# Hybrid mixer and mixture-of-experts layer: low parts of the merged sum first in the last output block, two weight slots in their space, expert tiles in that of the router and of the F ring

## The chip, the cores and the metric

The kernel runs on one core of a Trainium2 chip. The metric is the device time of one execution in microseconds (us); smaller is better. A kernel's time is the median of several runs.

## What is computed

One layer of a trunk over 512 latent tokens of width 1024, with 256 context tokens. Three token mixers (pooling, differential attention, RWKV-7) give three branches, which are merged with gates; an output projection of the merged sum is added to the stream; then a router picks for each token one group of experts out of four and the best two experts in it, and the two experts' outputs are added to the stream.

```python
def merge_branches(branches, gates, w_br, w_out):
    ...
    return merged @ w_out

def hier_moe(h, w_rg, w_re, w_g, w_u, w_d):
    ...                      # top-1 group of 4, top-2 of its 8 experts
    # block_ffn, for each expert e and its tokens:
    return (jax.nn.silu(xblk @ w_g[e]) * (xblk @ w_u[e])) @ w_d[e]

x = x + mod[:, 2] * mix_l                      # mix_l = merge_branches(...)
f_l = modulate(x, norm2_g[l], mod[:, 3], mod[:, 4])
x = x + mod[:, 5] * hier_moe(f_l, ...)
```

There are 32 experts; each has a gate and an up matrix of 1024 x 512 and a down matrix of 512 x 1024, all in 4-byte floats, so 6 MiB an expert and 192 MiB in all. Every expert is computed for 64 token slots.

## The kernel before

**Stages.** Up to about 892 us the input projection, the mixers and the merge run. From there the output projection runs (`out_mm`, line 1440), in four blocks of 256 output columns; each block is done for four groups `t` of 128 tokens. The merged sum is kept as a rounded high part `mgh` and a remainder `mgl`, and the weights of a block as `wo[i][0]` and `wo[i][1]` likewise; one group of one block takes 24 matmuls, for each of the eight pieces `k` of the inner dimension high by high, low by high and high by low. `out_add` (lines 1446 to 1452) adds the result to the stream `xt2` on VectorE. In the loops at lines 1553 to 1574 blocks 2 and 3 are mixed with the router: `turned` (line 1363) transposes the stream of a token group into a tile `fT`, `logits` (line 1370) multiplies it with the router's weights, `route` (lines 1374 to 1395) finds the experts, `count` (line 1403) the place of each token in its expert, and `normed` (lines 1428 to 1435) writes the normalised tokens to a tile `xn` and, through a tile `xf` and the ACT queue, to the array `x_d` in the chip's memory. `gates` (lines 1408 to 1421) is the router's last step. `gather(0)` (lines 1494 to 1525) picks the rows of the first four experts by matmuls (line 1500) and writes them to `xT`; for later groups of four the rows come from `x_d` by an indirect DMA (line 1535).

**Experts.** The loop at line 1701 runs over the experts: `up` (line 1602) multiplies `xT` with the gate matrix, then with the up matrix, `hidden` applies the activation, `turn_` transposes, `down` (line 1637) multiplies with the down matrix of the expert before, `combine` and `add` (lines 1645 to 1647) put the result back to the tokens.

**Expert weights.** Every matrix is loaded as two halves of 1 MiB (128 rows of 8 KB). `order` is the order of loads: the order in which the experts use them, but for two halves, 4 and 5 (`SPARE`, expert 0's down matrix). `fetch(n)` issues loads on the SP queue up to the n-th; load n goes to the slot `RING[n % 13]`. So 13 loads fit in the ring and two more in `SPARE` tiles: 15 halves before the experts begin. A load waits, on SP and in SP's order, until its slot's earlier user is through:

- slots 0 to 7 lie in `pea`, slot 12 in two tiles of the ring named F;
- slots 8 and 9 (`ew8`, `ew9`) lie in the space of `mgh`, pieces k = 0 to 3 and 4 to 7;
- slots 10 and 11 lie in the pool `peq`, which is opened at line 1588 after the pools of `mgl` (`mgx`) and of five F tiles (`pf_`) are closed; the F tiles hold at that time the four `fT` and then the four `xf`, from which `x_d` is written;
- the two `SPARE` halves go to the tiles `oh`, `yhl` and `xT` of the pool `ep` (line 1591), which the experts use later, and which lies where the router's tiles were, and beyond.

```python
RING = (4, 5, 6, 7, 12, 0, 1, 2, 3, 8, 9, 10, 11)
...
fetch(11)          # line 1583: slots 8 and 9
gates()
...
fetch(NS)          # line 1589: slots 10 and 11; NS is 13
```

**Order.** A planner with a model of the time puts the instructions of each engine into an order, by their place in the program and by the priorities given (`tc.high_priority`); it also places all semaphores. Each engine and each DMA queue then runs its list in order.

Of the kernel before, what the change touches and what calls it, by code (L numbers as in the profile page):

```python
# [77 lines left out]
def trunk_kernel(ctx: ExitStack, tc: tile.TileContext, I, out, dbg=None, upto=99):  # L78
# [65 lines left out]
    def ps_big(shape=(128, 512)):  # L144
        return ppool.tile(list(shape), FT, name="pp", bufs=5)
# [4 lines left out]
    def ps_sm(shape=(128, 512)):  # L150
        return psum.tile(list(shape), FT, name="psm", bufs=3)
# [588 lines left out]

    pb = ctx.enter_context(ExitStack())
    TW = dict(bufs=1, reuse_waits="tile")
    pf_ = ctx.enter_context(ExitStack())

    wfb = ctx.enter_context(tc.tile_pool(name="rmapg", side="right", **TW))
    wfa = pf_.enter_context(tc.tile_pool(name="rmapf", side="right", **TW))

    class Ring:
        n = 0
# [738 lines left out]
    def gather(b):  # L1488

        oh = (ep if b else xnp).tile([128, 4, EB, 64], FR, name="oh", bufs=1)  # L1490
        ohf = oh.rearrange("p t e s -> p t (e s)")

        def chosen(t):
            return V.tensor_tensor(oh[:, t], slot[:, t, b * EB:b * EB + EB, None].to_broadcast([128, EB, 64]),
                                   io1[:, None, :].to_broadcast([128, EB, 64]), OP.is_equal)

        def rows_of(p, k, ts):
            for t in ts:
                for a in range(2):
                    PE.matmul(p, xns[t // 2][:, a, t % 2, k * 128:k * 128 + 128], ohf[:, t], start=(t == 0 and a == 0),  # L1500
                              stop=(t == 3 and a == 1))

        def put(k, p):
            if k % 2:
                S.activation(xT[:, k], p, AF.Identity, scale=g2c[:, k:k + 1], bias=s2c[:, k:k + 1])
            else:
                V.tensor_scalar(xT[:, k], p, g2c[:, k:k + 1], s2c[:, k:k + 1], op0=OP.mult, op1=OP.add)

        if b == 0:

            ahead = {}
            for t in range(3):
                chosen(t)
                yield
            for k in range(AH):
                ahead[k] = ps_big()[:, 0:EB * 64]
                rows_of(ahead[k], k, range(3))
            chosen(3)
            yield
            xT = ep.tile([128, KD, EB * 64], FT, name="xT")  # L1520
            for k in range(KD):
                p = ahead[k] if k in ahead else ps_big()[:, 0:EB * 64]
                rows_of(p, k, (3,) if k in ahead else range(4))
                put(k, p)
            yield xT, *slots(b, oh)
            return
        for t in range(4):
            chosen(t)
        yield
        gc, ix = slots(b, oh)  # L1530
        ii = ep.tile([128, EB // 2], U32, name="ii")
        V.tensor_copy(ii, ix)
        fe = fes[b % 2]
        for q in range(EB // 2):
            G.indirect_dma_start(out=fe[:, q], out_offset=None, in_=x_d[:, :],
                                 in_offset=bass.IndirectOffsetOnAxis(ap=ii[:, q:q + 1], axis=0),
                                 bounds_check=L - 1, oob_is_err=False)
        yield
        xT = ep.tile([128, KD, EB * 64], FT, name="xT")
        for k in range(0, KD, 2):  # L1540
            p = ps_big()
            for i in range(2):
                for q in range(EB // 2):
                    c = 2 * i + q
                    PE.transpose(p[:, c * 128:c * 128 + 128], fe[:, q, (k + i) * 128:(k + i) * 128 + 128], ident)
            for i in range(2):
                put(k + i, p[:, i * 256:i * 256 + 256])
            if k == 2:
                yield
        yield xT, gc, ix  # L1550

    nxt = gather(0)
    for t in range(4):
        p = ps_big()[:, 0:256]
        for k in range(KD):
            out_mm(p, wo[2], t, k)
        turned(t, 0, 4)
        out_add(p, t, 2)
    for t in range(5):
        if t < 4:  # L1560
            p = ps_big()[:, 0:256]
            for k in range(KD):
                out_mm(p, wo[3], t, k)
            out_add(p, t, 3)
        if t:
            with tc.high_priority(0):
                turned(t - 1, 4, 4)
                logits(t - 1, 0, 8)
                if t > 1:
                    count(t - 2)  # L1570
                route(t - 1)
            normed(t - 1)
        if t > 1:
            next(nxt)
# [5 lines left out]
    if upto < 7:  # L1580
        return
    dump("slot", slot)
    fetch(11)
    gates()
    m2x.close()
    mgx.close()
    pf_.close()
    peq = ctx.enter_context(tc.tile_pool(name="expq", side="right", **TW))
    fetch(NS)
    epx = ctx.enter_context(ExitStack())  # L1590
    ep = epx.enter_context(tc.tile_pool(name="experts", bufs=2, reuse_waits="tile"))
# [7 lines left out]
    def up(xT, w, pg, i):  # L1599
        for k in range(KD):  # L1600
            for h in range(2):
                PE.matmul(pg[64 * h:64 * h + 64, i], xT[:, k], of(w[i], k)[:, h * 256:h * 256 + 256],  # L1602
                          start=(k == 0), stop=(k == KD - 1), tile_position=(0, 64 * h))

    def hidden(pg, pool):
# [40 lines left out]
        PE.matmul(p, oT[:, t * 128:t * 128 + 128], yl, start=False, stop=True)  # L1646
        V.tensor_add(xt2[t][:, sl], xt2[t][:, sl], p)  # L1647

    def parts_of(y, h, rows, pool, name="yhl", eng=G):

        sl = slice(h * 512, h * 512 + 512)
        yhl = pool.tile([rows, 2, 512], FR, name=name, bufs=1)
        yh, yl = yhl[:, 0], yhl[:, 1]
        S.activation(yh, y[:, sl], AF.Copy)  # L1654
        eng.tensor_sub(yl, y[:, sl], yh.bitcast(FT))  # L1655
        return sl, yh, yl

    def combine(y, ix, last=False):

        oT = oT_  # L1660
        V.tensor_scalar(oT, iol, ix, None, op0=OP.is_equal)
        if last:
            yield
            with tc.high_priority(100):
                pts = [parts_of(y, h, 128, ep, *(("oh", G) if h else ("yhl", V))) for h in range(2)]
            for h in range(2):
                sl, yh, yl = pts[h]
                for t in range(4):
                    add(oT, t, sl, yh, yl)
                    (nc.sync if t % 2 else nc.scalar).dma_start(out[t * 128:(t + 1) * 128, sl], xt2[t][:, sl])  # L1670
            return
        pt_ = parts_of(y, 0, 128, ep)
        yield
        for t in range(4):
            add(oT, t, *pt_)
        pt_ = parts_of(y, 1, 128, ep)
        yield
        for t in range(4):
            add(oT, t, *pt_)
# [1 line left out]
    def store(t):  # L1681
        nc.sync.dma_start(out[t * 128:(t + 1) * 128], xt2[t])

    load(SPARE[0], *(ep.tile([128, 1, D], FT, name=nm, bufs=1) for nm in ("oh", "yhl")))
    load(SPARE[1], ep.tile([128, 2, D], FT, name="xT"))
    cur = next(nxt)
    io_ = xnp.tile([128, 2, L], FR, name="oh", bufs=1)
    iol, oT_ = io_[:, 0].bitcast(FT), io_[:, 1]
# [12 lines left out]
    for e in range(NE + 1):  # L1701
        fetch(NS + max(0, 6 * e - 2) - (2 if e > 1 else 0))
        j = e % EB
        if e < NE:
            if j == 0:
                got[e // EB] = cur
                nxt = gather(e // EB + 1) if e + EB < NE else iter(())
            xT = got[e // EB][0][:, :, j * 64:j * 64 + 64]
            pg = ps_big().rearrange("p (i n) -> p i n", i=2)
            up(xT, weights(e), pg, 0)  # L1710
        elif com:
            next(com, None)
# [33 lines left out]
    with tc.If(nmost > 64):  # L1746
        for t in range(4):
            if t % 2 == 0:
                xns.append(xnp.tile([128, 2, 2, D], FR, name=f"xn{t // 2}"))
            xf = op_.tile([128, D], FT, name="xf")  # L1750
            nc.sync.dma_start(xf, x_d[t * 128:(t + 1) * 128])
            S.activation(xns[-1][:, 0, t % 2], xf, AF.Copy)
            V.tensor_sub(xns[-1][:, 1, t % 2], xf, xns[-1][:, 0, t % 2].bitcast(FT))
        with tc.For_i(0, NE, 1) as e:
# [12 lines left out]
            with tc.For_i(0, 7, 1):  # L1767
# [18 lines left out]
                y = op_.tile([64, D], FT)  # L1786
                pg = ps_big().rearrange("p (i n) -> p i n", i=2)
                up(xT, wo, pg, 0)
                up(xT, wo, pg, 1)
                down(turn_(hidden(pg, op_), op_), wo, gc, y, 0)  # L1790
                oT = op_.tile([64, 512], FR)
                pt = ps_sm()[0:64]
# [1 line left out]
                    PE.transpose(pt[:, t * 128:t * 128 + 128], oh[:, t].bitcast(FT), ident)  # L1794
                S.activation(oT, pt, AF.Copy)
                for h in range(2):
                    pt_ = parts_of(y, h, 64, op_)
                    for t in range(4):
                        add(oT, t, *pt_)
        for t in range(4):  # L1800
# [115 lines left out]
```

## Time and profile before

| | |
|---|---|
| median of 3 runs | 1446.18 us |
| the runs | 1446.18, 1440.47, 1446.46 us |
| profiled execution | 1446.82 us, of it 1444.7 us in the span of the trace |
| busy in the span | TensorE 1362.9 us (94%), VectorE 819.1 us, ScalarE 483.4 us, GpSimd 382.9 us |
| moved by DMA | 401.00 MB, mean 278 GB/s |
| granted TensorE clock, mean | 0.979 of full speed (2.4 GHz) |

The trace is that of one execution, so a sum is made against 1446.82 us, of which 2.1 us lie outside the span. All positions are microseconds from the start of the span. "PE" is TensorE's matmuls, "PEld" its weight loads, DVE VectorE, ACT ScalarE, POOL GpSimd; SPq and ACTq are the engines' DMA queues. A matmul's end is modelled, so "busy" of PE says that the engine had work, not that it ran at its peak. DMA share is the mean busy share of the 16 DMA engines.

### The profile page before, as it was taken

To read this page: it belongs to the slowest core of one execution; us is meant where nothing else is said; L and a number is where in the kernel's file an instruction comes from. 1 tells how busy PE (TensorE), PEld (TensorE's weight loads), DVE (VectorE), ACT (ScalarE), POOL (GpSimd) and SP (SyncE) were. 2 spreads that over 40 slices of the span, in tenths; PEclk is the share of its full clock that TensorE was granted. 3 is DMA by queue.
4 is the path that set the end of the run, shared out by engine and by line. 5 is a ranking of instruction groups with operands and counts; after the bars stand their busy time and mean duration, and the time that the engine had idled before them with its cause. 6 is when DMAs were issued, how large, how long until landed. Compare 5 with 4: busy or idle time off the path is not lost.

```text
span 1444.7 us, 24038 instructions
## 1 busy us (share of the span) xinstructions
PE 1362.9 (94%) x9148; PEld 1019.1 (71%) x9148; DVE 819.1 (57%) x1670; ACT 483.4 (33%) x1089; POOL 382.9 (27%) x345
## 2 busy tenths in 40 slices
PE   5999999999999998899999998999999999999897
PEld 3786788987888886788887777985555554555443
DVE  4553327779988948367776886462333433333324
ACT  4432235765565632243345524341111111111101
POOL 2111155445532442212221347111101101111001
PEclk9999999999999999899999999999999999999999
DMA  9368655666566466985847276579999999999996
GB/s 367 150 216 312 233 181 171 217 216 222 168 231 208 183 207 209 243 259 143 259 135 245 88 266 232 192 292 417 418 416 418 418 417 418 418 417 419 418 418 245
DMA packets 138614, 401.00 MB, mean 278 GB/s; under 512 B 38821, under 2 KB 69541, under 8 KB 107776
## 3 DMA queue, kind: packets, MB, share of 16 engines
q1 hardware_dynamic: 102640, 332.72, 62.5%
q10 hardware_dynamic: 32256, 58.47, 11.0%
q0 software_dynamic: 3600, 8.24, 1.7%
q8 instruction: 74, 1.21, 0.3%
q14 instruction: 44, 0.36, 0.1%
HBM read 344.47 MB, written 58.72 MB: 279 GB/s over the span
## 4 chain that ended last, share of the span: by engine, by line
PE 62%; DMA 21%; DVE 9%; issue 4%; ACT 2%; POOL 1%; SPq 1%; ACTq 0%; DVEq 0%; POOLq 0%
PE pp L219 13%; PE pp L1602 8%; DMA ew<-in_w_eu_dram 7%; PE pp L233 4%; PE pp L1637 4%; PE pp L1146 3%; PE pp L1440 3%; DMA ew<-in_w_ed_dram 3%; DMA ew<-in_w_eg_dram 3%; PE sc L1001 2%; PE pp L832 2%; PE pp L1645 1%; PE pp L820 1%; PE sc L1000 1%; PE pp L865 1%
## 5 line engine op out<-in xcount | busy, mean ns | idle before, releaser
L1602 PE MATMUL pp<-ew,xT 128*64 128x256 f32 x1888 | 225.1, 383 | 15.3 <-DMA ew<-in_w_eu_dram 10.1
L1602 PEld LDWEIGHTS pp<-ew,xT 128*64 128x64 f32 x1888 | 131.9, 137 | 98.5 <-issue 17.9
L219 PE MATMUL pp<-xlh,wh 128*128 128x512 f32 x344 | 137.2, 410 | 6.0 <-ACT wide L412 6.0
L219 PE MATMUL pp<-xll,wh 128*128 128x512 f32 x344 | 136.8, 398 | 0.4 <-POOL xll L319 0.4
L219 PE MATMUL pp<-xlh,wl 128*128 128x512 f32 x344 | 136.1, 396 | 0.0
L1655 POOL TENSOR_TENSOR yhl<-m,yhl 128x512 fp32r<-128x512 f32 x30 | 38.2, 1274 | 364.9 <-ACT yhl L1654 364.9
L214 POOL TENSOR_TENSOR wl<-wraw,wh 128x512 fp32r<-128x512 f32 x84 | 114.0, 1386 | 61.9 <-ACT wh L213 54.9
L1647 DVE TENSOR_TENSOR x<-x,pp 128x512 f32<-128x512 f32 x128 | 80.8, 681 | 44.4 <-PE pp L1646 44.4
L1637 PE MATMUL pp<-ew,hT 128*64 128x512 f32 x440 | 101.3, 599 | 0.0
L1608 DVE TENSOR_TENSOR hh<-hh,pp 128x256 f32<-128x256 f32 x32 | 13.5, 421 | 148.0 <-ACT hh L1607 148.0
L219 PEld LDWEIGHTS pp<-xlh,wh 128*128 128x128 f32 x344 | 65.4, 192 | 26.0 <-ACT wide L412 6.7
L1640 DVE SCALAR_TENSOR_TENSOR m<-pp,gc,m 64x512 f32<-64x512 f32 x62 | 46.5, 750 | 62.5 <-PE pp L1637 61.8
L213 ACT ACTIVATE wh<-wraw 128x512 fp32r<-128x512 f32 (+1 forms) x112 | 61.0, 612 | 49.2 <-PE pp L219 47.0
L219 PEld LDWEIGHTS pp<-xll,wh 128*128 128x128 f32 x344 | 66.0, 192 | 15.4 <-issue 2.0
L219 PEld LDWEIGHTS pp<-xlh,wl 128*128 128x128 f32 x344 | 65.9, 191 | 14.1
L1637 PEld LDWEIGHTS pp<-ew,hT 128*64 128x64 f32 x440 | 28.9, 136 | 55.5 <-issue 50.7
L233 PE MATMUL pp<-wh,xlh 128*128 128x256 f32 x192 | 60.2, 314 | 3.4 <-ACT qo L658 2.3
L1616 ACT ACTIVATE hT<-psm 128x256 f32<-128x256 f32 x32 | 12.3, 384 | 152.1 <-PE psm L1614 146.3
L801 POOL TENSOR_TENSOR ao<-ar,cst 128x512 f32<-128x512 f32 x24 | 31.1, 1295 | 115.9 <-PE pp L813 46.3
L1607 ACT ACTIVATE hh<-pp 128x256 f32<-128x256 f32 x32 | 12.3, 384 | 139.6 <-PE pp L1602 139.6
L233 PE MATMUL pp<-wl,xlh 128*128 128x256 f32 x192 | 58.3, 304 | 0.0
L233 PE MATMUL pp<-wh,xll 128*128 128x256 f32 x192 | 58.2, 303 | 0.0
(436 smaller groups left out, 3126.3 us busy)
## 6 DMA issues: line engine op xcount, KB each, us to landing
ew<-in_w_eg_dram SPq DMA_DIRECT2D x59, 1024.0 KB
ew<-in_w_eu_dram SPq DMA_DIRECT2D x58, 1024.0 KB
ew<-in_w_ed_dram SPq DMA_DIRECT2D x56, 1024.0 KB
wraw<-in_w_in_dram SPq DMA_DIRECT2D x27, 1024.0 KB
u_d<-ub ACTq DMA_DIRECT2D x16, 1152.0 KB
wada<-in_w_adr_dram SPq DMA_DIRECT2D x16, 1024.0 KB
ar<-u_d SPq DMA_DIRECT2D x24, 640.0 KB
wa<-in_w_ad_dram SPq DMA_DIRECT2D x8, 1024.0 KB
```

Of the source, the lines that this page charges most:

```text
L213: S.activation(self.h[:, kk, :n], raw[:, kk, :n], AF.Copy)
L214: (eng[q % 2] if type(eng) is tuple else eng).tensor_sub(self.l[:, kk, :n], raw[:, kk, :n], self.h[:, kk, :n].bitcast(FT))
L219: PE.matmul(ps, a[:, k, cs], b[part][:, k], start=(k + n == 0), stop=(k == KD - 1 and n == 2))
L233: PE.matmul(ps, a[part][:, k, ts], b[:, k], start=(n == 0), stop=(n == 3 * KD - 1))
L801: G.tensor_mul(ao, aa[:, :, 2:3].to_broadcast([128, 4, 2, 64]), offm[:, None].to_broadcast([128, 4, 2, 64]))
L1146: PE.matmul(ps, a[:, k], bs[k][:, x], start=(c == 0), stop=(c == 11))
L1440: PE.matmul(p, a[:, ts], x[:, k], start=(k == 0 and c == 0), stop=(k == KD - 1 and c == 2))
L1602: PE.matmul(pg[64 * h:64 * h + 64, i], xT[:, k], of(w[i], k)[:, h * 256:h * 256 + 256], start=(k == 0), stop=(k == KD - 1), tile_position= ...
L1637: PE.matmul(pd[64 * h:64 * h + 64], hT[:, k], of(w[2], k)[:, h * 512:h * 512 + 512], start=(k == 0), stop=(k == 3), tile_position=(0, 64 * h))
L1640: V.scalar_tensor_tensor(y[ps_, h * 512:h * 512 + 512], pd[64 * h:64 * h + 64], gc, m5[ps_, h * 512:h * 512 + 512], op0=OP.mult, op1=OP.mult)
L1647: V.tensor_add(xt2[t][:, sl], xt2[t][:, sl], p)
L1655: eng.tensor_sub(yl, y[:, sl], yh.bitcast(FT))
```

## The change

- In block 3 the products low by high are taken out of the group loop and done first, ahead of block 2, into four accumulators `pss`; block 3's loop then does only high by high and high by low, 16 matmuls a group instead of 8 + 16. Block 2's accumulators for t = 1 to 3 come from the other accumulator pool. No matmul is added or removed.
- `mgx` is closed right behind block 2, and `peq` opened in its space; slots 10 and 11 come ahead of 8 and 9 in `RING`, and their loads (`fetch(11)`) are issued ahead of block 3.
- The F tiles' pool stays open. `xT` is kept as two halves in F tiles (two sets, four tiles), the fifth F tile takes half a `SPARE` load and then `yhl`. `ep` becomes smaller by these.
- The second `SPARE` load goes out as two transfers of 512 KB instead of one of 1 MiB.
- In the branch for more than 64 tokens an expert, tiles come from F as well; the trace of before shows no work of that branch.

```diff
@@ -740,10 +740,9 @@
-    pf_ = ctx.enter_context(ExitStack())
...
-    wfa = pf_.enter_context(tc.tile_pool(name="rmapf", side="right", **TW))
+    wfa = ctx.enter_context(tc.tile_pool(name="rmapf", side="right", **TW))
@@ -1217,7 +1216,7 @@
-    RING = (4, 5, 6, 7, 12, 0, 1, 2, 3, 8, 9, 10, 11)
+    RING = (4, 5, 6, 7, 12, 0, 1, 2, 3, 10, 11, 8, 9)
@@ -1501,10 +1500,11 @@
         def put(k, p):
+            x = xT[k // 4][:, k % 4]
...
-            xT = ep.tile([128, KD, EB * 64], FT, name="xT")
+            xT = xTs[b % 2]
@@ -1550,18 +1550,27 @@
     nxt = gather(0)
+
+    pss = [ps_big()[:, 0:256] for _ in range(4)]
     for t in range(4):
-        p = ps_big()[:, 0:256]
+        for k in range(KD):
+            PE.matmul(pss[t], mgl[k][:, t * 128:t * 128 + 128], wo[3][0][:, k], start=(k == 0), stop=False)
+    for t in range(4):
+        p = (ps_sm() if t else ps_big())[:, 0:256]
         for k in range(KD):
             out_mm(p, wo[2], t, k)
         turned(t, 0, 4)
         out_add(p, t, 2)
+    mgx.close()
+    peq = ctx.enter_context(tc.tile_pool(name="expq", side="right", **TW))
+    fetch(11)
     for t in range(5):
         if t < 4:
-            p = ps_big()[:, 0:256]
             for k in range(KD):
-                out_mm(p, wo[3], t, k)
-            out_add(p, t, 3)
+                for c in range(2):
+                    PE.matmul(pss[t], mgh[k][:, t * 128:t * 128 + 128], wo[3][c][:, k], start=False,
+                              stop=(k == KD - 1 and c == 1))
+            out_add(pss[t], t, 3)
@@ -1580,15 +1589,15 @@
-    fetch(11)
     gates()
     m2x.close()
-    mgx.close()
-    pf_.close()
-    peq = ctx.enter_context(tc.tile_pool(name="expq", side="right", **TW))
     fetch(NS)
     epx = ctx.enter_context(ExitStack())
     ep = epx.enter_context(tc.tile_pool(name="experts", bufs=2, reuse_waits="tile"))
+
+    spare = wfa.tile([128, 1, D], FT, name="F", bufs=7 - FB)
+    xTs = [[wfa.tile([128, KD // 2, EB * 64], FT, name="F", bufs=7 - FB) for _ in range(2)] for _ in range(2)]
+    yhl_ = []
@@ -1681,8 +1695,8 @@
-    load(SPARE[0], *(ep.tile([128, 1, D], FT, name=nm, bufs=1) for nm in ("oh", "yhl")))
-    load(SPARE[1], ep.tile([128, 2, D], FT, name="xT"))
+    load(SPARE[0], ep.tile([128, 1, D], FT, name="oh", bufs=1), spare)
+    load(SPARE[1], *(x.rearrange("p (o k) n -> p o (k n)", o=1) for x in xTs[1]))
...
```

## Rows read from the trace of the kernel before

**Rows 1.** Windows of the expert stage: length, busy us of PE, PEld, DVE, ACT, POOL, clock, DMA share, GB/s

```profile
966.50:1169.00 202.50, 200.88 (x1407) 113.75 (x1408) 77.69 (x146) 28.16 (x58) 27.11 (x23) 1.00 1.02 417
1169.00:1402.00 233.00, 217.62 (x1460) 116.72 (x1458) 82.09 (x148) 29.12 (x61) 25.99 (x22) 1.00 1.01 418
```

**Rows 2.** Chain that ended last, expert stage: start, us, what

```profile
1027.89 3.45 PE pp L1602 x32
...
1084.05 3.45 PE pp L1602 x32
...
1384.33 17.45 DMA ew<-in_w_eu_dram
1401.82 1.95 PE pp L1602 x16
```

**Rows 3.** Windows of DMA ahead of the experts, same columns as in Rows 1

```profile
926.00:940.00 14.00, 14.00 (x122) 14.00 (x121) 5.70 (x18) 5.68 (x14) 0.55 (x1) 1.00 0.01 4
...
946.00:957.50 11.50, 10.98 (x91) 10.16 (x89) 9.78 (x57) 6.61 (x12) 0.60 (x2) 1.00 0.91 331
957.50:959.50 2.00, 1.72 (x16) 1.60 (x16) 1.76 (x11) 0.16 (x1) 0.00 (x0) 1.00 0.04 14
959.50:971.00 11.50, 11.50 (x102) 10.05 (x103) 6.45 (x16) 3.98 (x6) 3.56 (x2) 1.00 0.96 372
```

**Rows 4.** Timeline of the SP queue: start, us, engine, line, operation

```profile
919.40 0.33 SPq L1251 DMA_DIRECT2D ew<-in_w_eu_dram  x1
919.78 0.95 SPq L1251 DMA_DIRECT2D ew<-in_w_eg_dram  x1
946.22 0.33 SPq L1251 DMA_DIRECT2D ew<-in_w_eg_dram  x1
948.54 10.76 SPq L1251 DMA_DIRECT2D ew<-in_w_eu_dram  x2
959.41 0.36 SPq L1251 DMA_DIRECT2D ew<-in_w_ed_dram  x1
959.90 0.35 SPq L1251 DMA_DIRECT2D oh<-in_w_ed_dram  x1
...
968.50 0.34 SPq L1251 DMA_DIRECT2D ew<-in_w_ed_dram  x1
...
981.51 5.84 SPq L1251 DMA_DIRECT2D ew<-in_w_eg_dram  x2
```

**Rows 5.** Waits of the SP queue, 900 to 1000: total us, times, longest

```profile
SPq L1251 <- PE pp L1440: 43.9, 4, 25.4
...
SPq L1251 <- DMA x_d<-F: 10.0, 1, 10.0
```

**Rows 6.** Timeline of PE: block 2's first matmul, the transposes behind its first group, two later steps

```profile
919.33 0.28 PE L1440 MATMUL pp<-xn,ew 128*128 128x256 f32 x1
...
922.18 0.60 PE L1363 MATMUL psm<-cst,x 128*128 128x128 f32 x4
...
962.57 1.06 PE L1738 MATMUL psm<-rt,cst 128*128 128x32 f32 x8
...
966.51 3.24 PE L1602 MATMUL pp<-ew,xT 128*64 128x256 f32 x28
```

**Rows 7.** Two windows as in Rows 1, and the sum of 919.3 to 966.5

```profile
935.50:948.50 13.00, 13.00 (x115) 13.00 (x114) 8.26 (x30) 8.17 (x15) 1.64 (x3) 1.00 0.30 101
948.50:960.30 11.80, 11.00 (x89) 10.06 (x88) 10.63 (x59) 5.62 (x11) 0.55 (x1) 1.00 0.75 276
...
sum 47.20, PE 46.40 PEld 45.34 DVE 27.86 ACT 20.01 POOL 2.47; mean PE 7.73 PEld 7.56 DVE 4.64 ACT 3.33 POOL 0.41
```

**Rows 8.** Timeline of DVE: block 3's first addition, the router's last step

```profile
935.53 0.42 DVE L1446 TENSOR_TENSOR tm<-pp,m 128x256 f32<-128x256 f32 x1 [1.42 <-PE pp L1440]
...
959.59 0.28 DVE L1421 TENSOR_TENSOR tg<-oo 128x128 f32<-128x128 f32 x1
```

**Rows 9.** A window behind the load issued at 919.40, same columns as in Rows 1

```profile
920.00:922.00 2.00, 2.00 (x19) 2.00 (x19) 0.57 (x2) 0.51 (x2) 0.00 (x0) 1.00 0.73 193
```

More of the change, by code (lines that the diff above doesn't have):

```diff
@@ L1503, in put @@
         def put(k, p):
+            x = xT[k // 4][:, k % 4]
             if k % 2:
-                S.activation(xT[:, k], p, AF.Identity, scale=g2c[:, k:k + 1], bias=s2c[:, k:k + 1])
+                S.activation(x, p, AF.Identity, scale=g2c[:, k:k + 1], bias=s2c[:, k:k + 1])
             else:
-                V.tensor_scalar(xT[:, k], p, g2c[:, k:k + 1], s2c[:, k:k + 1], op0=OP.mult, op1=OP.add)
+                V.tensor_scalar(x, p, g2c[:, k:k + 1], s2c[:, k:k + 1], op0=OP.mult, op1=OP.add)
         if b == 0:
@@ L1538, in gather @@
         yield
-        xT = ep.tile([128, KD, EB * 64], FT, name="xT")
+        xT = xTs[b % 2]
         for k in range(0, KD, 2):
@@ L1601, in up @@
             for h in range(2):
-                PE.matmul(pg[64 * h:64 * h + 64, i], xT[:, k], of(w[i], k)[:, h * 256:h * 256 + 256],
+                PE.matmul(pg[64 * h:64 * h + 64, i], xT[k], of(w[i], k)[:, h * 256:h * 256 + 256],
                           start=(k == 0), stop=(k == KD - 1), tile_position=(0, 64 * h))
@@ L1647, in add, with parts_of @@
         V.tensor_add(xt2[t][:, sl], xt2[t][:, sl], p)
-    def parts_of(y, h, rows, pool, name="yhl", eng=G):
+    def parts_of(y, h, yhl, eng=G):
+        if yhl is yhl_:
+            if not yhl_:
+                yhl_.append(wfa.tile([128, 2, 512], FR, name="F", bufs=7 - FB))
+            yhl = yhl_[0]
         sl = slice(h * 512, h * 512 + 512)
-        yhl = pool.tile([rows, 2, 512], FR, name=name, bufs=1)
         yh, yl = yhl[:, 0], yhl[:, 1]
@@ L1664, in combine @@
             with tc.high_priority(100):
-                pts = [parts_of(y, h, 128, ep, *(("oh", G) if h else ("yhl", V))) for h in range(2)]
+                pts = [parts_of(y, h, ep.tile([128, 2, 512], FR, name="oh", bufs=1) if h else yhl_, G if h else V)
+                       for h in range(2)]
             for h in range(2):
@@ L1671, in combine @@
             return
-        pt_ = parts_of(y, 0, 128, ep)
+        pt_ = parts_of(y, 0, yhl_)
         yield
@@ L1675, in combine @@
             add(oT, t, *pt_)
-        pt_ = parts_of(y, 1, 128, ep)
+        pt_ = parts_of(y, 1, yhl_)
         yield
@@ L1707, in trunk_kernel @@
                 nxt = gather(e // EB + 1) if e + EB < NE else iter(())
-            xT = got[e // EB][0][:, :, j * 64:j * 64 + 64]
+            xT = [got[e // EB][0][k // 4][:, k % 4, j * 64:j * 64 + 64] for k in range(KD)]
             pg = ps_big().rearrange("p (i n) -> p i n", i=2)
@@ L1749, in trunk_kernel @@
                 xns.append(xnp.tile([128, 2, 2, D], FR, name=f"xn{t // 2}"))
-            xf = op_.tile([128, D], FT, name="xf")
+            xf = wfa.tile([128, D], FT, name="F", bufs=7 - FB)
             nc.sync.dma_start(xf, x_d[t * 128:(t + 1) * 128])
@@ L1785, in trunk_kernel @@
                 V.tensor_copy(gc, pi)
-                y = op_.tile([64, D], FT)
+                y = wfa.tile([128, D], FT, name="F", bufs=7 - FB)[0:64]
                 pg = ps_big().rearrange("p (i n) -> p i n", i=2)
-                up(xT, wo, pg, 0)
-                up(xT, wo, pg, 1)
+                up([xT[:, k] for k in range(KD)], wo, pg, 0)
+                up([xT[:, k] for k in range(KD)], wo, pg, 1)
                 down(turn_(hidden(pg, op_), op_), wo, gc, y, 0)
@@ L1796, in trunk_kernel @@
                 for h in range(2):
-                    pt_ = parts_of(y, h, 64, op_)
+                    pt_ = parts_of(y, h, wfa.tile([128, 2, 512], FR, name="F", bufs=7 - FB)[0:64])
                     for t in range(4):
```

## Prediction

> **What bounds the kernel now.** I read the page's slices first, then windows, then the chain. From 966.5 us, where the first expert starts, the 16 DMA engines are full: share 1.02 and 417 GB/s up to 1169, 1.01 and 418 GB/s up to 1402 [rows 1]. The reader is to see that PE also looks busy there, but that the chain that ended last changes: up to about 1169 its pieces are PE's, an expert taking (1084.05 - 1027.89) / 4 = 14.0 us, and the last wait for a weight ends at 1401.82, behind a piece that is a DMA's from 1384.33 on [rows 2]. One expert's weights, 6 x 1.0486 MB at 418 GB/s, take 15.05 us, over PE's 14.0. So the stage is set by DMA: PE begins with 15 halves in store, eats them up, and then follows the transfers. The end moves by as much as the unbroken stream of weights is moved, and by nothing else. So the question is where that stream begins, and what it has behind it when it begins.
>
> It begins at 959.5. Between 926 and 940 the DMA engines stand nearly still (4 GB/s), from 946 to 957.5 they carry 331 GB/s, from 957.5 to 959.5 14 GB/s, and then 372 GB/s up to 971 [rows 3]. The SP queue tells why. After the load of 919.78 nothing goes out until 946.22 (slot 8) and 948.54 (slot 9), then nothing until 959.41 (slots 10 and 11), then the two SPARE loads from 959.90 on, and the first slot that an expert gives back is filled at 968.50 [rows 4]. SP waited at line 1251 for the output projection's matmuls 25.4 us at the longest, and once 10.0 us for the write `x_d<-F` [rows 5]: that is the place of slots 10 and 11, which must wait for the last `xf`.
>
> **The change, part by part.**
>
> *Loads for slots 10 and 11 (two halves, 2.51 us each) leave earlier.* One group of block 2 takes 24 matmuls in 922.18 - 919.33 = 2.85 us, 0.119 us each [rows 6]. Block 3's 32 low products, put first, take 3.8 us, so block 2's four groups end at 932.0 + 3.8 = 935.8 (932.0 is 919.33, four times 2.85, and some 0.4 for each of the three sets of transposes between them). `mgl`'s first four pieces are last read some 13 matmuls before that, at 934.3. So the two loads leave at about 934.4 and 936, in place of 946.22 and 948.54 for the tenth and eleventh, into idle DMA, and are in by 942. Behind them on SP stand only the loads of slots 8 and 9, which wait for block 3's end (948.54) anyway; ACT's queue, with the writes of `x_d`, is not SP's.
>
> *Slots 8 and 9 take the next two loads,* at block 3's end as before. So from 946 to 957.5 the same bytes flow as before: two halves, the writes of `x_d`, a constant. The wait of 10.0 us on `x_d` is gone.
>
> *What is late next.* The SPARE loads: `oh` lies where the router's tiles were, whose last reader ends at 959.59 + 0.28 = 959.87 [rows 8], and before, `oh` was issued at 959.90 [rows 4], so this very wait already ended last for it. The F tiles' last user (`x_d`, up to 958.9, by the 10.0 us behind 948.9) is earlier. So they still leave at 959.9. Behind them the ring is full: 13 + 2 halves are all there is room for, before and after, and the next load leaves only when expert 0 gives back its first half, at 968.50 [rows 4].
>
> *So the gain is not two loads (5.0 us) but the queue that stood at 968.50.* Before: from 959.5 to 971 flowed 11.5 us x 372 GB/s = 4.28 MB [rows 3]; the four halves are 4.19 MB, so they end 0.2 us before 971, at 970.8, and the stream goes on unbroken. At 418 GB/s they need 10.0 us, so the first of them began in effect at 960.8, 1.4 us behind its issue at 959.41. The load of 919.40 gives 1.7: by 922 it had moved 2 x 193 = 0.39 MB, 0.9 us of full rate [rows 4, 9]. I take 1.4, since it is the same stage; the range is 1.4 to 1.7. After: the SPARE halves flow from 961.3 to 966.3, the engines then idle, and the stream begins with the load of 968.50 at 969.9 (970.2 by the other price). It begins 970.8 - 969.9 = 0.9 us earlier (0.6 at least), if expert 0 starts when it did.
>
> The Trainium skill, DMA: Bandwidth & Descriptors, section "Latency and other measured facts", gives about 0.6 us to the first byte for queues of this kind. By it the stream would begin at 969.1, and the gain would be 1.7 us; the rows, with 1.4 and 1.7 us to the full rate, don't bear that out.
>
> *Is the stream unbroken afterwards?* The ninth load behind 968.50 leaves at 981.51 + 5.84 - 0.33 = 987.0 [rows 4]; the stream, now from 969.9, reaches it at 969.9 + 8 x 2.51 = 990.0, and it needs 1.4 us of start: 1.6 us in hand. Later PE gives slots back every 14.0 / 6 = 2.34 us against 2.51, so the margin grows.
>
> *Does expert 0 start when it did?* From 919.3 to 966.5 PE is busy 46.40 of 47.20 us [rows 7], and no matmul is added or taken out, so it can start 0.8 us earlier at most, and 0.9 us more if the planner moves the token totals (line 1738, from 962.57 for 0.9 us) behind it [rows 6]. Later: block 3's first group now ends at 935.8 + 0.4 + 16 x 0.119 = 938.1, so the first addition, at 935.53 before [rows 8], comes 2.8 us later, and DVE, which then has the routing, is busy 10.63 of 11.8 us at the end [rows 7]. But from 935.5 to 948.5 it had 13.0 - 8.26 = 4.7 us to spare, more than 2.8, and the last group's addition comes no later. I take 0, between -1.7 and +2.8.
>
> *The rest.* The second SPARE load as two transfers costs SP 0.33 us more, in a stretch with 2 us to spare before 968.50. Block 2 now shares the smaller accumulator pool with the transposes, each freed by an addition or a copy a group (3 us) earlier. `xT` in halves and one `yhl` for all experts leave the same readers to wait for, in a stage where DMA ends last: 0.
>
> **The rivals.**
>
> *Two whole loads are gained.* If the stream gained all that went into the idle stretch, 5.0 us: 1446.18 - 5.0 = 1441.2. For it: DMA bounds the stage and 926 to 940 is empty. Against it: the ring is full at 966.3, and expert 0 would have to start 4 us earlier, which PE's 0.8 us of idle time excludes.
>
> *DVE becomes the bound ahead of the experts, and the kernel gets slower.* Place: the routing from 938 to 960. Price: up to the 2.8 us by which DVE starts later; the stream then begins at 968.50 + 2.8 + 1.4 = 972.7, 1.9 us later than before: 1448.1. It decides from a delay of 0.9 us on. For it: DVE's 90% at the end. Against it: its 4.7 us of slack ahead.
>
> *The change doesn't do what it says:* the planner puts the low products late, or mixes them into block 2, and the loads leave at 946 as before. Then four halves and `x_d` flow from 946, 3.8 + 2.1 MB, at 418 GB/s 14.1 us and so up to 961.5, the SPARE halves up to 966.5, still ahead of 968.50: the same 0.9 us. Only if the wait on `x_d` also stayed would it be 0, 1446.2. So the early departure is spare; the lifted wait is the gain.
>
> **How the numbers follow.** Forecast: 0.9 us less than the profiled 1446.82, 1445.9; the median of the runs lies 0.64 below that execution, so 1446.18 - 0.9 = 1445.3. Its own range is with expert 0 up to 1.7 us earlier (2.6 in all, 1443.6) and with no gain (1446.2). Chances: 0.66 for that; 0.22 for the slower rival; 0.06 for two whole loads; 0.06 for no effect. The range reaches up to 1448.1. Down, it takes in 1441.2, and the runs' own scatter: one of three stood at 1440.47, 5.7 below the median; a median of such runs, less 0.9, is 1439.6. So 1439.6 to 1448.1. About 0.5% is what a measurement of this kernel can tell from no change; that is 7.2 us, below 1438.9 or above 1453.4, and no case here goes so far. I leave 0.04 on each side for what I haven't seen, 0.92 for within.
>
> **What would show it.** Right: two loads between 934 and 937 on SP, the next two near 948, no wait for `x_d<-F` there; SPARE loads still near 960; DMA idle between about 966.5 and 970; the first slot refilled within 1.5 us of 968.5; rates of 418 GB/s from 970 on. Wrong: SPARE loads ahead of 955 together with expert 0 ahead of 964 (more gain); expert 0 behind 967.5 with PE idle for DVE between 945 and 960 (a loss); DMA idle again between 985 and 1005, which would say that the slots, not the transfers, bound the beginning.

## The result, and the profile after

| | before | after |
|---|---|---|
| median of the runs | 1446.46 us (21 runs, 1440.47 to 1450.88) | 1454.17 us (21 runs, 1448.83 to 1465.49) |
| ratio | | 1.0063, 95% interval 1.0046 to 1.0081 |
| profiled execution | 1446.82 us, span 1444.7 | 1448.83 us, span 1447.0 |
| mean granted clock of the profiled execution | 0.979 | 0.979 (others of the same kernel: down to 0.967) |

I had forecast 1445.3 us and a range up to 1448.1; it became some 9 us slower by the ratio (0.0063 x 1446.5; the two medians differ by 7.7). The profiled execution of after is the fastest of its 21; the repeat of it below, 1459.72 us, is one of the longer ones.

The 21 executions of after differ together with TensorE's clock: the seven below 1451 us have a mean granted clock of 0.976 to 0.979, the four above 1460 one of 0.967 to 0.969.

Executions differ by some microseconds in where the projection begins, so I count from a mark that all traces have: the load that leaves at the end of block 1, 919.40 before [rows 4] and 917.23 after. The first slot came back 968.50 - 919.40 = 49.1 us behind it before, and 970.46 - 917.23 = 53.2 after. SP's timeline of after (start, us, engine, line, operation), to be read beside [rows 4]:

```profile
917.23 0.33 SPq L1250 DMA_DIRECT2D ew<-in_w_eu_dram  x1
917.61 16.45 SPq L1250 DMA_DIRECT2D ew<-in_w_eg_dram  x2
934.11 9.78 SPq L1250 DMA_DIRECT2D ew<-in_w_eu_dram  x2
944.53 0.33 SPq L1250 DMA_DIRECT2D ew<-in_w_ed_dram  x1
953.21 3.88 SPq L1250 DMA_DIRECT2D F<-in_w_ed_dram  x3
960.63 0.33 SPq L1250 DMA_DIRECT2D oh<-in_w_ed_dram  x1
970.46 0.33 SPq L1250 DMA_DIRECT2D ew<-in_w_ed_dram  x1
```

The loads do what the change says: the second of the row of 917.61 goes out at about 933.7, the next at 934.11; before, the loads at these two places in the order left at 946.22 and 948.54 [rows 4]. Then the queue waits for the experts, from 960.63 to 970.46. SP's waits of after, 900 to 1000 (total us, times, longest), beside [rows 5]: the wait on `x_d` has moved from the ring to the SPARE loads, which lie in F tiles now.

```profile
SPq L1250 <- DMA x_d<-F: 10.8, 2, 8.2
```

The expert stage is nearly as in [rows 1], 412 and 418 GB/s against 417 and 418; the 412 has the start with empty engines in it, and from 997.23 to 1169 it is 417 (windows of after: length, busy us of PE, PEld, DVE, ACT, POOL, clock, DMA share, GB/s). Ahead of it, from the mark to 80 us behind it, first before and then after:

```profile
970.46:1169.00 198.54, 197.09 (x1372) 110.10 (x1370) 75.28 (x146) 25.31 (x54) 24.75 (x21) 1.00 1.01 412
1169.00:1402.00 233.00, 218.54 (x1464) 117.08 (x1462) 83.06 (x150) 30.17 (x63) 26.33 (x22) 1.00 1.02 418
```

```profile
919.40:999.40 80.00, 77.65 (x629) 64.44 (x628) 37.62 (x137) 25.28 (x53) 8.62 (x9) 1.00 0.72 284
```

```profile
917.23:997.23 80.00, 77.24 (x615) 64.93 (x616) 35.76 (x135) 24.26 (x51) 8.11 (x8) 0.96 0.70 261
```

284 GB/s x 80 us are 22.72 MB, 261 are 20.88: after is 1.84 MB behind, at 418 GB/s 4.4 us. From the mark to the end of the span it needs 529.8 us against 525.3: 4.5 more. All that is lost is lost ahead of the full stream. Where, the windows of 944 to 976 of after show:

```profile
944.00:948.00 4.00, 3.99 (x37) 3.88 (x35) 3.87 (x12) 3.71 (x7) 0.00 (x0) 1.00 0.86 279
948.00:952.00 4.00, 1.91 (x9) 1.94 (x10) 3.87 (x23) 2.74 (x4) 0.56 (x1) 0.73 0.96 344
952.00:956.00 4.00, 4.00 (x32) 3.89 (x31) 1.79 (x10) 0.83 (x2) 0.00 (x0) 0.84 1.07 407
956.00:960.00 4.00, 3.33 (x28) 3.02 (x27) 3.93 (x32) 0.43 (x2) 0.00 (x0) 1.00 0.86 279
960.00:964.00 4.00, 4.00 (x24) 4.00 (x23) 2.18 (x8) 0.66 (x2) 0.00 (x0) 0.57 0.64 208
964.00:968.00 4.00, 4.00 (x36) 4.00 (x36) 1.48 (x6) 1.04 (x2) 0.00 (x0) 1.00 0.02 4
968.00:972.00 4.00, 4.00 (x37) 2.59 (x35) 2.47 (x2) 2.37 (x3) 3.56 (x2) 1.00 0.20 33
```

PE is busy only 1.91 of 4 us in the second window, and the granted clock falls: 0.73, 0.84 and 0.57 are means of its two levels, 2.4 and 1.2 GHz. Before, it was 1.00 there [rows 7]. It falls while PE still stands, and a second time near 960.1, where PE is busy (its 1-us window 0.55, the one ahead of it 1.00):

```profile
949.00:950.00 1.00, 0.00 (x0) 0.00 (x0) 0.96 (x9) 1.00 (x3) 0.00 (x0) 0.93 0.78 221
```

PE's timeline of after names the wait (in brackets: idle us before, and who ended it); line 1402 is `count`, line 1394 the last step of `route`:

```profile
944.33 3.66 PE L1369 MATMUL pp<-wg__8941,F 128*128 128x36 f32 x32
950.09 0.60 PE L1402 MATMUL psm<-rt,cst 128*128 128x32 f32 x2 [2.10 <-DVE rt L1394]
...
968.47 3.24 PE L1611 MATMUL pp<-ew,F 128*64 128x256 f32 x28
```

And DVE's timeline, of after and then of before, says why `rt` was late:

```profile
936.21 0.42 DVE L1445 TENSOR_TENSOR tm<-pp,m 128x256 f32<-128x256 f32 x1 [0.47 <-PE pp L1571]
...
940.00 1.29 DVE L1430 SCALAR_TENSOR_TENSOR xn<-x,ss,xn 128x1024 fp32r<-128x1024 f32 x1 [1.01 <-ACT xn L1429]
...
944.12 1.28 DVE L1430 SCALAR_TENSOR_TENSOR xn<-x,ss,xn 128x1024 fp32r<-128x1024 f32 x1 [1.15 <-ACT xn L1429]
...
946.49 1.26 DVE L1430 SCALAR_TENSOR_TENSOR xn<-x,ss,xn 128x1024 fp32r<-128x1024 f32 x1
...
949.75 0.19 DVE L1394 TENSOR_TENSOR rt<-oo 128x32 f32<-128x32 f32 x1
```

```profile
947.83 0.19 DVE L1395 TENSOR_TENSOR rt<-oo 128x32 f32<-128x32 f32 x1
...
950.00 1.28 DVE L1431 SCALAR_TENSOR_TENSOR xn<-x,ss,xn 128x1024 fp32r<-128x1024 f32 x1 [0.16 <-ACT xn L1430]
```

Block 3's first addition stands 18.98 us behind the mark (936.21 - 917.23), before 16.13 [rows 8]: 2.85 later. Then three `xn` steps stand ahead of `rt`, where before the third came behind it: 1.26 more. Together that is 4.11; `rt` came 32.52 us behind the mark against 28.43, 4.09 later. PE was done with the work in front of `count` at 947.99, 30.76 behind the mark, as before (before, it began `count` at 950.05, 30.65 behind), and `rt` had then been ready for 2.0 us. So a reserve of 2.0 us (the time by which `rt` had been ready ahead of PE) met a delay of 4.1: a wait of 2.1.

### The profile page after: what moved, and what is told of

It reads as the page before. It is cut to its first block, busy times and chain, and to the rows that moved or that the text cites. A ratio compares the mean times of both kernels' runs of the same rounds, so it can differ in the third digit from the quotient of the medians.

```text
span 1447.0 us, 24050 instructions
## 1 busy us (share of the span) xinstructions
PE 1361.4 (94%) x9148; PEld 1015.4 (70%) x9148; DVE 821.6 (57%) x1670; ACT 483.1 (33%) x1089; POOL 383.2 (26%) x345
## 4 chain that ended last, share of the span: by engine, by line
PE 62%; DMA 17%; DVE 12%; issue 3%; ACT 3%; SPq 1%; POOL 1%; ACTq 0%; DVEq 0%; POOLq 0%
PE pp L219 14%; PE pp L1611 8%; DMA ew<-in_w_eu_dram 7%; PE pp L1646 4%; PE pp L1145 4%; PE pp L233 3%; DMA ew<-in_w_eg_dram 3%; DMA ew<-in_w_ed_dram 3%; PE pp L1439 2%; PE pp L1654 2%; DVE ptmp L617 2%; PE sc L1000 2%; PE pp L819 1%; PE sc L999 1%; PE pp L864 1%
## 5 line engine op out<-in xcount | busy, mean ns | idle before, releaser
L1611 PE MATMUL pp<-ew,F 128*64 128x256 f32 x1888 | 225.3, 383 | 14.7 <-DMA ew<-in_w_eu_dram 9.9
L1611 PEld LDWEIGHTS pp<-ew,F 128*64 128x64 f32 x1888 | 131.0, 137 | 99.0 <-issue 17.6
L1668 POOL TENSOR_TENSOR F<-m,F 128x512 fp32r<-128x512 f32 x30 | 38.2, 1272 | 364.1 <-ACT F L1667 360.4
L1617 DVE TENSOR_TENSOR hh<-hh,pp 128x256 f32<-128x256 f32 x32 | 13.5, 422 | 150.9 <-ACT hh L1616 150.9
L1625 ACT ACTIVATE hT<-psm 128x256 f32<-128x256 f32 x32 | 12.3, 384 | 154.3 <-PE psm L1623 148.4
L1616 ACT ACTIVATE hh<-pp 128x256 f32<-128x256 f32 x32 | 12.3, 385 | 142.8 <-PE pp L1611 142.8
```

What stands on the lines that cost most here:

```text
L1611: PE.matmul(pg[64 * h:64 * h + 64, i], xT[k], of(w[i], k)[:, h * 256:h * 256 + 256], start=(k == 0), stop=(k == KD - 1), tile_position=(0, ...
```

## The experiments

For each profiled execution, from its trace: the time from the mark to the first slot given back; the PE waits of 0.3 us and more from 944 us to that slot; how long the clock was at its lower level in that stretch (from 1-us windows); and by how much the bytes of the first 80 us (mean rate x 80) fall short of before's 22.72 MB, at 418 GB/s, beside the growth of the time from the mark to the end of the span (before 525.3).

| kernel | ratio (95%) | first slot | PE waits | at 1.2 GHz | short by | longer by |
|---|---|---|---|---|---|---|
| before | | 49.1 | none (0.28 longest) | 0 | 0 | 0 |
| e1 before again | 1.0003 (0.9984 to 1.0023) | 49.9 | none (0.28) | 3.4 | 1.3 | 2.0 |
| after | 1.0063 (1.0046 to 1.0081) | 53.2 | 2.10, 0.38 | 6.8 | 4.4 | 4.5 |
| e2 after again | 1.0066 (1.0039 to 1.0093) | 61.5 | 2.10 | 27.3 | 12.6 | 12.7 |
| e3 reorder only | 1.0092 (1.0066 to 1.0119) | 61.6 | 2.10 | 27.3 | 12.6 | 12.9 |
| e4 space only | 1.0017 (0.9995 to 1.0038) | 49.1 | none (2.12 behind it) | 0 | 1.7 | 1.9 |
| e5 count later | 1.0056 (1.0029 to 1.0082) | 60.6 | 0.83, 0.69 | 27.3 | 11.7 | 11.5 |
| e6 in turn | 1.0074 (1.0046 to 1.0103) | 60.4 | 1.29, 0.67, 0.43 | 23.9 | 11.1 | 11.2 |
| e8 filler | 1.0034 (1.0013 to 1.0056) | 55.7 | 1.11, 1.03 | 6.8 | 6.7 | 7.1 |
| e11 late route | 1.0098 (1.0064 to 1.0132) | 62.6 | 5.03, 0.79 | 23.9 | 13.8 | 13.9 |
| e12 space, select late | 0.9983 (0.9966 to 1.0001) | 49.1 | none (0.28) | 0 | 0.2 | 1.1 |
| e15 the same again | 0.9996 (0.9975 to 1.0017) | 49.1 | none (0.28) | 0 | 0.2 | 1.1 |
| e13 filler, more | 1.0032 (1.0016 to 1.0048) | 53.7 | 0.75 | 0 | 4.6 | 5.5 |
| e14 before with that filler | 1.0051 (1.0029 to 1.0072) | 57.7 | 0.82 | 6.8 | 8.8 | 8.4 |

"First slot" to "longer by" are microseconds; "none (2.12 behind it)" means that the wait came behind the first slot. The last two columns agree within 1 us in every row: the end follows the bytes that are missing when the stream is full.

**Both kernels again, and the two halves of the change.** The reorder alone is the kernel before with these lines of the change. The space alone is the change without them, with slots 8 and 9 first and with the loads and the pool `peq` at their places of before, behind block 3:

```diff
# e3, against before
+    pss = [ps_big()[:, 0:256] for _ in range(4)]
     for t in range(4):
-        p = ps_big()[:, 0:256]
+        for k in range(KD):
+            PE.matmul(pss[t], mgl[k][:, t * 128:t * 128 + 128], wo[3][0][:, k], start=(k == 0), stop=False)
+    for t in range(4):
+        p = (ps_sm() if t else ps_big())[:, 0:256]
...
-                out_mm(p, wo[3], t, k)
-            out_add(p, t, 3)
+                for c in range(2):
+                    PE.matmul(pss[t], mgh[k][:, t * 128:t * 128 + 128], wo[3][c][:, k], start=False,
+                              stop=(k == KD - 1 and c == 1))
+            out_add(pss[t], t, 3)
# e4, against after: the same lines the other way round, and
-    RING = (4, 5, 6, 7, 12, 0, 1, 2, 3, 10, 11, 8, 9)
+    RING = (4, 5, 6, 7, 12, 0, 1, 2, 3, 8, 9, 10, 11)
```

> The kernel before, unchanged, for the granted clock of each execution beside its span. If the loss of the changed kernel is one of TensorE's clock, the executions of this one keep a mean clock near the 0.979 of its profile, with spans within 1440 to 1451 us; if its clock also wanders down to 0.967 as the changed kernel's did, the clock doesn't tell the two apart.

> The changed kernel, unchanged. Order theory (block 3 shrinks, PE runs out of work in front of the count of the first token group, waits 2.1 us, and the granted clock falls behind that): ratio 1.004 to 1.008, and in the profile a PE wait of about 2 us between 945 and 952 followed by a stretch at about half the clock. Space theory (the expert tiles in F cost waits in the expert stage): the same ratio, but the loss lies behind 1000 us.

> The kernel before with only the order of block 3's products changed: low parts first, slots and tiles as before. Order theory: slower, by as much as the changed kernel or 1 us more, ratio 1.004 to 1.009, with the PE wait of about 2 us in front of line 1403's first matmuls and a fall of the clock. Space theory: ratio 1.000, within 1 us of before.

> The changed kernel with block 3's products in the order of before: slots 10 and 11 in the space of mgl, expert tiles in F, loads for slots 8 and 9 first. Order theory: no PE wait, expert 0 starts as in before, and the lifted wait on x_d gives what the prediction said, 0.9 us less than before, ratio 0.999 (0.997 to 1.000). Space theory: ratio 1.004 to 1.008 like the changed kernel.

The kernel before, run again, keeps mean clocks of 0.973 to 0.984; the repeat of after has 0.968 to 0.978. The reorder alone is as slow as the change, or slower; for the space alone no loss is shown. In the repeat of after the wait is the same 2.10 us as in the first trace, but the clock stays down four times as long, 27.3 us against 6.8 (PE's row, then windows):

```profile
952.72 0.61 PE L1402 MATMUL psm<-rt,cst 128*128 128x32 f32 x2 [2.10 <-DVE rt L1394]
```

```profile
952.00:980.00 28.00, 27.00 (x128) 26.50 (x130) 12.22 (x65) 5.51 (x12) 1.18 (x1) 0.51 0.46 161
```

In the space alone the gain was missing all the same. PE stands in the middle of expert 0, because DVE has the first select (line 1668, which writes `oh`) ahead of the last two `put`s (line 1507, which write the rows to `xT`'s F tiles):

```profile
971.72 0.65 PE L1605 MATMUL pp<-ew,F 128*64 128x256 f32 x4 [2.12 <-DVE F L1507]
```

```profile
968.43 2.79 DVE L1668 TENSOR_SCALAR oh<-oh,ix 128x512 fp32r<-128x512 f32 x1 [3.21 <-ACT oh L1699]
971.14 0.98 DVE L1507 TENSOR_SCALAR F<-pp,g2c,s2c 128x256 f32<-128x256 f32 x2
```

**Is it the clock?** Two ways to have the change without the wait (the count a step later; block 3 group by group behind block 2's), one that fills the wait with work, and one that makes `rt` late in the kernel before:

```diff
# e5, against after
-                if t > 1:
-                    count(t - 2)
                 route(t - 1)
             normed(t - 1)
+                if t > 2:
+                    count(t - 3)
...
# e6, against after
-    for t in range(4):
-        p = (ps_sm() if t else ps_big())[:, 0:256]
...
     for t in range(5):
         if t < 4:
+            p = (ps_sm() if t else ps_big())[:, 0:256]
+            for k in range(KD):
+                out_mm(p, wo[2], t, k)
+            turned(t, 0, 4)
+            out_add(p, t, 2)
...
# e8, against after
+                if t == 2:
+                    idle_ = ps_sm()[:, 0:256]
+                    for k in range(24):
+                        PE.matmul(idle_, mgh[k % KD][:, 0:128], wo[3][0][:, k % KD], start=(k == 0), stop=(k == 23))
                 if t > 1:
                     count(t - 2)
# e11, against before
-        V.tensor_add(rt[:, t], oo[:, t, 0], oo[:, t, 1])
+        [V.tensor_add(rt[:, t], oo[:, t, 0], oo[:, t, 1]) for _ in range(1 if t else 16)]
```

> The changed kernel, with the count of each token group issued one step later, so that TensorE, which takes its instructions in order, has the next group's transposes and logits in front of the first count. Nothing is added or left out. Clock theory (the loss is a 2.1 us wait of TensorE for rt, behind which its granted clock falls): no wait above 1 us ahead of line 1402, granted clock above 0.95 in every 4 us from the start of block 2 to expert 0, first slot given back 48 to 50 us behind block 2's start (before: 49.1; the change: 53 to 62), ratio to before 0.998 to 1.002. Rival (the routing chain on VectorE and ScalarE is itself too late): the wait only moves to the next count or to the gathers, 53 us and more, ratio 1.004 to 1.009.

> The changed kernel, with block 3's products of a token group right behind block 2's of the same group, so that the additions come every 4.8 us and not in a burst of one in 2 us at the end; the low products still come first, slots 10 and 11 are still filled early. Nothing is added or left out. Clock theory: TensorE waits for rt less than 1 us, granted clock above 0.95 throughout, first slot given back 47.5 to 49.5 us behind block 2's start, loads ahead of 960 as in the change, and then the gain that I had forecast: ratio 0.998 to 1.001. Rival (space and early loads cost the time in another place): ratio 1.004 to 1.009.

> The changed kernel with 24 more products (24 x 0.119 = 2.9 us of TensorE work) into an accumulator that nobody reads, in front of the first count: more work, less waiting. Clock theory: the work takes the place of the 2.1 us wait, the granted clock stays above 0.95 from 944 to 980 us, first slot given back 49 to 51 us behind block 2's start, ratio 0.999 to 1.003, so that added work makes it faster than the change. Rival (the routing chain is late by itself, and the clock is a by-product): 2.9 us are added or at best hidden, ratio 1.006 to 1.009, as the change or worse.

> The kernel before, whose routing result rt of token group 0 is written 16 times in place of once (each 0.12 to 0.19 us of VectorE, the same value), so that rt comes some 3 us later and TensorE waits for it 1.5 to 3 us at line 1403, with the order of the output projection and all loads as before. Clock theory: the granted clock falls to 0.5 to 0.6 for 8 us or more behind that wait, first slot given back 53 us or more behind block 2's start, ratio 1.004 to 1.010. Rival (the wait costs its own length, the clock stays): 1 to 3 us, first slot given back 50 to 52 us behind it, ratio 1.000 to 1.002.

The two rearrangements failed: their waits are shorter (0.83, 1.29) but the clock fell, and for longer than in the first trace of after. In e6 the early loads were lost as well: behind the load of 919.42 none left until 946.40. So neither shows the change without the wait. In e5 the clock fell ahead of the wait, with PE busy in every one of the microseconds 940 to 947, 40 products of 36 columns and four transposes being the last of it (PE's rows, then the windows around the fall):

```profile
942.38 1.87 PE L1369 MATMUL pp<-wg__8941,F 128*128 128x36 f32 x16
944.08 0.64 PE L1362 MATMUL psm<-cst,x 128*128 128x128 f32 x4
944.55 3.26 PE L1369 MATMUL pp<-wg__8941,F 128*128 128x36 f32 x24
948.65 0.61 PE L1402 MATMUL psm<-rt,cst 128*128 128x32 f32 x2 [0.83 <-DVE rt L1394]
```

```profile
944.00:946.00 2.00, 2.00 (x21) 2.00 (x20) 1.99 (x9) 2.00 (x5) 0.00 (x0) 1.00 0.99 410
946.00:948.00 2.00, 1.81 (x12) 1.67 (x11) 1.65 (x15) 1.49 (x4) 0.56 (x1) 0.69 0.94 287
948.00:974.00 26.00, 24.67 (x114) 24.07 (x116) 12.63 (x65) 3.92 (x9) 0.84 (x1) 0.50 0.47 169
```

So my wording, that the clock falls behind a 2.1 us wait, is too narrow. The late `rt` in the kernel before did what the clock theory said: order and loads untouched, a wait of PE (5.03 us, more than the 1.5 to 3 that I meant), and the clock at 0.51 up to 968, from 954.4 on, within that wait and behind it. The first slot came 13.5 us later than in before, where PE's two waits are 5.8 us together, so the waits' own length is not the price:

```profile
954.00:968.00 14.00, 10.17 (x48) 10.20 (x49) 8.17 (x49) 3.96 (x7) 0.55 (x1) 0.51 0.71 262
```

The filler made the change faster by adding work (1.0034 against 1.0063 and 1.0066; the intervals overlap), but the clock still fell for 6.8 us behind two waits of 1.1 and 1.0 us further on. Hence the next run, with 12 more unread products ahead of each of those two places, and its control, the same 48 in the kernel before.

```diff
# e13, against e8; e14 is the kernel before with the lines of both
+                if t > 2:
+                    more_ = ps_sm()[:, 0:256]
+                    for k in range(12):
+                        PE.matmul(more_, xns[t - 3 >> 1][:, 0, (t - 3) % 2, 0:128], xns[t - 3 >> 1][:, 0, (t - 3) % 2, 0:256], start=(k == 0), stop=(k == 11))
                 if t > 1:
                     count(t - 2)
```

> The changed kernel with 48 products of 256 columns that nobody reads (5.7 us of TensorE work), 24 in front of the first count as in the run with the filler, 12 in front of each of the two gathers' first rows. Clock theory: no wait of TensorE above 0.7 us between 944 us and expert 0, granted clock 1.00 throughout, first slot given back 49 to 52.5 us behind block 2's start, ratio 0.999 to 1.003, although 5.7 us of work are added: below the 1.0034 with 24 and the 1.0063 with none. Rival (the clock falls for another reason than TensorE's waits and narrow products, or the added work costs its length): ratio 1.004 to 1.008.

> The control for the run with 48 unread products: the same 48 in the kernel before. There TensorE waits only 0.25 + 0.23 + 0.28 us, so 48 x 0.119 = 5.7 us of work can hide in 0.8 us at most: expert 0 gives back its first slot 54 to 54.9 us behind block 2's start in place of 49.1, the granted clock stays at 1.00, ratio 1.0030 to 1.0042. If it comes out so, equal to the 1.0032 of the change with the same products, then at an equal clock the change costs nothing and brings nothing that can be measured. Rival: ratio 1.000 to 1.002, that is, the products are mostly hidden, and the change with them still loses 2 us or more by itself.

With 5.7 us of useless work the clock stays at 1.00 up to the first slot, and the ratio goes from 1.0063 to 1.0032 (the ends of the intervals just overlap), although the first slot comes 1.2 us later than the latest that I expected:

```profile
944.00:972.00 28.00, 27.25 (x235) 26.79 (x236) 19.03 (x90) 12.33 (x24) 2.92 (x4) 1.00 0.63 236
```

In the control the clock fell, against what I expected, some 2 us behind a wait of 0.82 us, with one of 0.24 ahead of that; the first slot (57.7) and the ratio (1.0051) lie above what I expected, 54 to 54.9 and at most 1.0042 (windows ahead of the fall and with it):

```profile
957.00:963.00 6.00, 4.81 (x38) 4.29 (x37) 5.55 (x31) 1.22 (x4) 0.00 (x0) 1.00 0.84 314
963.00:971.00 8.00, 8.00 (x43) 7.76 (x44) 1.80 (x7) 1.15 (x3) 0.87 (x1) 0.57 0.83 291
```

So waits alone, by their length, don't say when it falls: 0.82 with a fall here, 0.75 without one in e13. What the two show together is the size: with equal useless work the change is not slower than the kernel before (1.0032 and 1.0051, overlapping intervals), as far as can be told while the clock fell in the traced execution of the one and not of the other. The other executions seem to go the same way: the median of their mean clocks is 0.977 in e14 against 0.981 in the runs of the kernel before taken with it, and 0.9795 in e13, as in those taken with that. So the size of the change at an equal clock stays open.

**Would the 0.9 us have come?** The space alone, with one more VectorE step of 128 x 1 that makes the select wait for the last `put`, run twice:

```diff
-                com = com if d == end else combine(y, ix[:, q:q + 1])
+                ixc = ix[:, q:q + 1]
+                if d == 1:
+                    ixc = ep.tile([128, 1], FT, name="ixc", bufs=1)
+                    V.scalar_tensor_tensor(ixc, got[0][0][1][:, 3, 0:1], 0.0, ix[:, q:q + 1], op0=OP.mult, op1=OP.add)
+                com = com if d == end else combine(y, ixc)
```

> The space change alone (block 3 in its old order, slots 8 and 9 filled first), with one more VectorE operation of 128 x 1 that makes the first select of line 1668 depend on the last piece of xT, so that it can't stand ahead of the last put. My theory: the wait of 2.12 us in expert 0 goes, the granted clock is 1.00 from block 2 to expert 1, the slots come back every 2.3 us from 49 us behind block 2's start on, and the stream of weights begins about 0.9 us earlier than in the kernel before: ratio 0.998 to 1.0005, below the 1.0017 with the wait. Rival (the SPARE loads in F tiles, or xT in two tiles, cost more than the wait): ratio 1.001 to 1.004, with another wait in expert 0.

> The space change with the late select once more, unchanged, since its ratio 0.9983 (0.9966 to 1.0001) left open whether it is faster than the kernel before. Its trace showed the first slot 49.1 us behind block 2's start, as before, then 266 and 307 GB/s for 8 us: by that there is no gain over a microsecond, ratio 0.999 to 1.001. Rival: it is faster by 2 us or more, ratio below 0.999 again, and the trace's one execution missed it.

The wait is gone, the clock is 1.00 up to the first slot, and expert 0 gives that back where it did before. The two ratios leave a gain of 1 us as possible as none. The trace of e12 speaks against one: the first slot came back at 967.75, and 8 us later the engines were not yet full (windows):

```profile
964.00:968.00 4.00, 4.00 (x38) 3.14 (x37) 0.99 (x3) 2.11 (x4) 2.52 (x2) 1.00 0.67 268
968.00:972.00 4.00, 4.00 (x40) 3.33 (x39) 1.33 (x1) 0.71 (x1) 1.05 (x1) 1.00 0.80 266
972.00:976.00 4.00, 4.00 (x41) 3.32 (x38) 0.42 (x1) 0.38 (x1) 0.00 (x0) 1.00 0.91 307
976.00:980.00 4.00, 4.00 (x36) 2.95 (x34) 0.00 (x0) 0.38 (x1) 0.00 (x0) 1.00 1.02 430
```

This version has the lowest ratios of all, and it is not shown to be faster than the kernel before.

## Why the prediction was wrong

*Right.* DMA bounds the expert stage, and the end moves with the stream: the table's last two columns. The two loads leave at 933.7 and 934.1 (forecast 934.4 and 936). Of the SPARE loads, all forecast for 959.9, three pieces left from 953.21 on and only `oh` at 960.63. Then the ring is full, and DMA idles until expert 0 gives back its first half (4 GB/s from 964 to 968 in after): the early departure is spare, as forecast.

*The step that failed* is "Does expert 0 start when it did?" with its "I take 0, between -1.7 and +2.8". Its first half was right: block 3's first addition comes 2.8 us later (measured 2.85). Its second half set that against DVE's idle time, "4.7 us to spare" in a window of 13 us. But a sum of idle time is no reserve of one chain. The reserve was to be read at the place where PE meets `rt`: 947.83 + 0.19 against 950.05 in the trace of before, 2.0 us. Two things more were left out: the planner may put another 1.26 us step (`xn`) ahead of the routing, as it did here, and ACT's `xn`, for which DVE waited 1.01 and 1.15 us, was not looked at.

*The price of the rival.* "DVE becomes the bound ahead of the experts" was the right direction and place, with 0.22, and its delay was 4.1 us, not 2.8. But the slowdown of some 9 us isn't the delay either: it has the granted clock in it, a term that my sum doesn't have. I had read the clock as 1.00 in every row, and not as something that could move. In the repeat of after PE's wait is 2.1 us and expert 0 gives back its first slot 12.4 us late, behind 27.3 us at 1.2 GHz; in after's first trace 4.1 us late, behind 6.8. That the low clock, not the order, makes the difference between these two is plain, since it is the same program. That the order brings it on is shown by e3, and that a late `rt` alone brings it on, by e11.

The Trainium skill, TensorE: Matmul & The Clock Gate, section "A second HAM failure mode: psum-queue depth-cycling", tells of a kernel whose TensorE pauses briefly and often between groups of matmuls, so that its clock goes back and forth between two levels. The traces agree in part: eight of the eleven falls between the mark and the first slot came within a pause of PE of 0.8 to 5.0 us or some 2 us behind one at the most. They differ in the other three: e5's, with no pause ahead of it, and e1's and the second of after, with pauses of 0.38 us at the most ahead.

*The 0.9 us.* Here the mechanism was right (the wait on `x_d` lifted, the stream's start set by the first slot), and the term mis-sized is the start of the stream: 1.4 us behind the first load, and unbroken from there, was too little. In e12 the slot came back at 967.75; from 969.15 (1.4 later) to 80 us behind its mark, 998.66, an unbroken stream would carry 29.5 us x 418 GB/s = 12.3 MB. Measured, from 48 us behind the mark on, some bytes from before 969.15 among them:

```profile
966.66:998.66 32.00, 30.24 (x233) 19.03 (x230) 9.19 (x21) 4.94 (x10) 5.26 (x5) 1.00 0.94 372
```

372 GB/s x 32 us are 11.9 MB: at least 0.4 MB or 1.0 us short. The window of 972 to 976 above alone lacks as much, (418 - 307) x 4 = 0.44 MB. The slots come back one by one to engines with nothing queued, where before, some of the four halves were still to come at 968.50, and the share stood at 0.96 to 1.02 [rows 1, 3]. That takes back the 0.9.

The estimate of 1.7 us that I had set beside it, by the first-byte figure of the Trainium skill, DMA: Bandwidth & Descriptors, section "Latency and other measured facts", is farther off still: e12's trace shows no gain at all.

*Open.* What decides when the clock falls: e13 and e14 have nearly the same longest wait, and only one fell. And what decides how long it stays down: 6.8 and 27.3 us for the same program.

## What to carry to other kernels

Where an in-order engine meets the result of a chain on other engines, read the reserve at that meeting (result ready against engine there), not from busy shares; an order that brings one engine's work forward eats that reserve. Where a change gives TensorE a new wait, put a price on it that holds the clock as well: here a wait of 2.1 us came with a first slot 4 to 12 us late. And where buffers are refilled only as they are consumed, as these slots are, ask what is still queued when the first comes back: here filling them earlier showed no gain.

## What I had not expected of the hardware

- The granted clock goes to 0.50 and stays there for 3.4 to 27.3 us in a stretch in which PE is busy nearly all the time: in e5 24.67 of 26 us at 0.50.
- It can fall while the trace shows no gap of PE, within a run of 40 products of 36 columns and four transposes (e5, between 946 and 947).
- The kernel before has it too at times: in e1's trace 3.4 us at the lower level between 958 and 963, with no wait above 0.28 us, and the first slot 0.8 us later.
